# Modulation weights in buffers of their own, a reordered opening, and layer 1's recurrence values formed side by side

## The chip, the cores and the metric

The kernel runs on one core of one Trainium2 chip. The metric is the device time of one execution in microseconds (us); lower is better. The span in a profile is the part of that time between the first and the last instruction of the profiled execution.

## The reference

The reference is a block of two layers (`DEPTH` = 2) for a stream of 512 latent tokens and 256 context tokens, `D_MODEL` = 1024, all in float32. What is computed, cut to what matters here:

```python
silu_c, silu_cc = jax.nn.silu(c), jax.nn.silu(c_ctx)
for l in range(DEPTH):
    mod_lat = jnp.split((silu_c @ ada_w[l] + ada_b[l])[:, None, :], 6, axis=-1)   # ada_w[l]: 1024 x 6144
    mod_ctx = jnp.split(silu_cc @ ada_w[l] + ada_b[l], 6, axis=-1)
    z_lat = jnp.split(_modulate(x, norm1_w[l], mod_lat[0], mod_lat[1]) @ w_in[l], SPLIT_POINTS, axis=-1)
    z_ctx = ...                                  # the same for the context tokens
    # three mixers: gated recurrence (reads q, f, i, g columns of z), neighbourhood attention, short convolution
    x = x + mod_lat[2] * _branch_merge(...)      # three branch gates, branch projections, w_out
    x = x + mod_lat[5] * _sq_relu_mlp(_modulate(x, norm2_w[l], mod_lat[3], mod_lat[4]), mlp_w1[l], mlp_w2[l])
    ...                                          # the context tokens likewise, in layer 0 only
# _modulate(x, w, shift, scale) = rmsnorm(x) * w * (1 + scale) + shift
```

So the six modulation vectors of a layer (shift, scale and gate of the mixers, 0 to 2; shift, scale and gate of the MLP, 3 to 5) come from a 1024 x 6144 matrix times two vectors, and each is needed at a different place of the layer. The recurrence's values are the 512 `i` columns of `w_in`.

## The kernel before

**Products.** Each float32 product is made of three products of reduced inputs: a weight slab (128 x 1024, fetched as one transfer of 512 KB) is split into `wh` (copied by ScalarE, L205) and `wl` (what is left, made by VectorE, L206); activations likewise into `Hh` and `Hl`, or, inside the MLP, into the two halves of a tile `S`. `fm` (L224) then issues, for each of 8 blocks of the contracted dimension, `wh` x hi, `wh` x lo and `wl` x hi: 24 matrix instructions for 512 latent columns (tile `pl`) and 24 for 256 context columns (tile `pc`). This pair is called a step below. `tm_in` (L247) has the roles turned round: tokens are stationary, and 256 columns of weights stream past.

**Slabs.** `slab_plan` (L25) lists all slabs in the order of use. `next_w` (L209) hands out slab n, has slab n+1 split and the transfers up to slab n+3 issued, and then, if its argument `step` is true, advances the modulation stream by one item. Raw slabs lie in three buffers with the tag `raw` (L177). A slab's pair lies in `wh` and `wl` (two buffers each); a few named slabs use other tiles (`slabs_in`, L89).

**The modulation stream.** `ada_stream` (L352) works through items of 512 KB, each a quarter of the columns of one modulation vector and half of the contracted dimension. At its step i it issues item i's transfer into a `raw` buffer, multiplies item i-1 on VectorE (`ada`, L376: for each of four blocks and each of one or two rows one SCALAR_TENSOR_TENSOR, L387, the first one L385; after each second item a transpose and a reduction, L394 and L395), and closes a column quarter with a small TensorE product (`ada_sum`, L399). Layer 0's stream (vectors 2, 4, 3, 5) runs from the convolution stage on; layer 1's (1, 0, 2, 4, 3, 5) from the last four slabs of the first quarter of layer 0's MLP hidden units on. For layer 0, and for vectors 0 and 1 of layer 1, there are two rows (latent and context), for the others of layer 1 one.

**The opening.** Vectors 0 and 1 of layer 0 are needed at once. `start` (L299) computes them on TensorE: `ada_block` (L270) fetches 512 KB (8 blocks of 128 x 128, rows of 512 bytes) for each of 8 column blocks and 2 vectors into a ring of six `S` tiles and issues its matrix instructions (L282); `ada_block_sum` (L286) closes a column block (L290, L292, L294, L296). Beside that `norm_sq` (L433) sums the squares of x over eight blocks (ScalarE L442, VectorE L443), `norm_rms` (L445) makes the reciprocal root (TensorE L452, a chain of thirteen small VectorE instructions, then L458 spreads it on a diagonal), `norm_bc` (L462) broadcasts it by TensorE (L466), and `norm_apply` (L472: L481, L483, L484) makes `Hh` and `Hl`. The first half of the recurrence's value columns is then formed block by block (L338) as `Hh` and `Hl` come.

**Between the layers.** `last_products` (L1080) ends layer 0's MLP with the context columns first, normalises these, and leaves the latent columns' normalisation as `pending`. In layer 1 `hgrn_v` (L492) calls `tm_in` once for each half of the 512 value columns; `tm_in` does the context tiles (t = 4, 5), then calls `settle`, which runs what is pending, then does the four latent tiles, the tile loop outside the loop over the contracted dimension. In `mlp` (L1117) the hidden units go in quarters e = 0 to 3: eight `mlp_w1` steps with the square (`square`, L1105: L1112 to L1115), then eight `mlp_w2` steps with the residual (L1027).

**Order.** The instructions are put in order per engine ahead of time, by a planner that follows the program's order, a priority, and its own estimate of when data is there. On the chip each engine and each issuing queue (SP issues nearly all transfers) runs its list strictly in order, so an instruction that waits holds all behind it.

## Time and profile before

| | |
|---|---|
| median of 3 runs | 2505.33 us (2498.78 to 2507.31) |
| the profiled execution's own time | 2507.57 us |
| its span | 2505.8 us |
| TensorE matrix instructions | 2459.6 us busy, 98% of the span |
| TensorE weight loads | 2111.3 us, 84% |
| VectorE (DVE) | 1475.4 us, 59% |
| ScalarE (ACT) | 812.6 us, 32% |
| mean transfer rate | 93 GB/s |

The profile gives, for each engine, the busy time; matrix instructions are pipelined and their ends are modelled, so an engine shown as busy can still lose time: the distance between the starts of two equal pieces of work tells more than the busy share. "Idle before, releaser" is the time for which an engine stood still ahead of an instruction, and what ended it. In a row of the timeline the columns are the start in us, the duration in us, the engine, the line, the operation, output<-inputs, the shapes and how many are merged in the row (x).

### The profile page before, as it was taken

Reading aid. Unit: us, or ns where it says so; the run is one execution under the profiler, and the core shown is the slowest. Engines: PE = TensorE matmul, PEld = TensorE weight load, DVE = VectorE, ACT = ScalarE, POOL = GpSimd, SP = SyncE. Lnnn points to the kernel's source line nnn. Section 1 sums busy time; section 2 is a strip of 40 time slices with the busy share of each in tenths; the row PEclk is TensorE's granted clock in tenths of the full one; section 3 lists DMA queues with packets and bytes.
Section 4 is the critical chain, followed back from the end, with each engine's and each line's share of the span. In section 5 each row is a group of like instructions: output and inputs, shape, how many; then the busy total and the mean of one; then the engine's idle time right before and its main releaser. Section 6 shows DMA issues by size and latency. Waiting matters only on the chain.

```text
span 2505.8 us, 40660 instructions
## 1 busy us (share of the span) xinstructions
PE 2459.6 (98%) x17040; PEld 2111.3 (84%) x17040; DVE 1475.4 (59%) x2952; ACT 812.6 (32%) x1435; POOL 28.0 (1%) x52
## 2 busy tenths in 40 slices
PE   7999999999999999999999999999999999999999
PEld 6888988888888888878888888888878888888887
DVE  6477867776664666675655464787653335634433
ACT  4334365321212233121222333445442223422322
POOL 0000000000000000000000000000000000000000
PEclk9999999999999999999999999999999999999999
DMA  8111112233334212333343222111222233222322
GB/s 267 60 44 45 51 53 69 77 118 118 93 118 143 76 60 85 116 113 125 120 132 119 93 76 74 52 61 49 66 74 97 97 126 108 77 94 93 101 93 93
DMA packets 112344, 233.32 MB, mean 93 GB/s; under 512 B 8224, under 2 KB 65824, under 8 KB 112160
## 3 DMA queue, kind: packets, MB, share of 16 engines
q1 hardware_dynamic: 111584, 229.14, 28.1%
q8 instruction: 134, 2.20, 0.4%
q10 hardware_dynamic: 576, 1.57, 0.2%
q14 instruction: 50, 0.41, 0.1%
HBM read 226.49 MB, written 4.19 MB: 92 GB/s over the span
## 4 chain that ended last, share of the span: by engine, by line
PE 86%; DVE 7%; DMA 5%; ACT 2%; issue 1%; SPq 0%; DVEq 0%; ACTq 0%
PE pl L239 55%; PE pc L239 15%; PE tp L263 4%; DMA ada<-in_ada_w 4%; PE pc L263 2%; DVE adac L387 2%; DVE wl L206 1%; PE av L853 1%; PE ho L645 1%; PE sc L888 1%; PE kvp L621 1%; PE ptp L934 1%; PE lv L551 1%; DVE S L590 1%; PE tp L338 1%
## 5 line engine op out<-in xcount | busy, mean ns | idle before, releaser
L205 ACT ACTIVATE wh<-raw 128x1024 fp32r<-128x1024 f32 x297 | 314.5, 1059 | 849.7 <-PE pl L239 379.2
L239 PE MATMUL pl<-Hh,wh 128*128 128x512 f32 (+1 forms) x1488 | 586.5, 394 | 0.5 <-DVE S L1002 0.5
L239 PE MATMUL pl<-Hh,wl 128*128 128x512 f32 (+1 forms) x1488 | 581.4, 391 | 3.9 <-DVE wl L206 3.9
L239 PE MATMUL pl<-Hl,wh 128*128 128x512 f32 (+1 forms) x1488 | 581.1, 391 | 0.0
L206 DVE TENSOR_TENSOR wl<-raw,wh 128x1024 fp32r<-128x1024 f32 x297 | 363.2, 1223 | 318.5 <-ACT wh L205 313.7
L239 PE MATMUL pl<-S,wh 128*128 128x512 f32 x1392 | 436.4, 395 | 2.9 <-ACT S L1114 2.8
L239 PEld LDWEIGHTS pl<-Hh,wl 128*128 128x128 f32 x1488 | 279.7, 188 | 67.8 <-DVE wl L206 7.0
L239 PEld LDWEIGHTS pl<-Hh,wh 128*128 128x128 f32 x1488 | 279.7, 188 | 57.0 <-issue 0.8
L239 PEld LDWEIGHTS pl<-Hl,wh 128*128 128x128 f32 x1488 | 279.8, 188 | 55.1 <-issue 0.5
L239 PEld LDWEIGHTS pl<-S,wh 128*128 128x128 f32 x1392 | 258.3, 188 | 57.8 <-ACT S L1114 3.2
L239 PE MATMUL pl<-S,wl 128*128 128x512 f32 x696 | 273.8, 393 | 0.0
L387 DVE SCALAR_TENSOR_TENSOR adac<-ada,sc,adac 128x256 f32<-128x256 f32 x448 | 196.4, 481 | 119.4 <-DMA ada<-in_ada_w 116.6
L239 PE MATMUL pc<-Hh,wh 128*128 128x256 f32 x872 | 244.2, 280 | 0.8 <-ACT wh L205 0.6
L239 PE MATMUL pc<-Hh,wl 128*128 128x256 f32 x872 | 244.2, 280 | 0.2 <-DVE wl L206 0.2
L239 PE MATMUL pc<-Hl,wh 128*128 128x256 f32 x872 | 244.2, 280 | 0.0
L239 PEld LDWEIGHTS pc<-Hh,wh 128*128 128x128 f32 x872 | 164.5, 189 | 5.8 <-ACT wh L205 0.8
L239 PEld LDWEIGHTS pc<-Hl,wh 128*128 128x128 f32 x872 | 164.6, 189 | 4.4 <-DVE Hl L484 0.2
L1027 DVE SCALAR_TENSOR_TENSOR S<-pl,mod,S 128x512 f32<-128x512 f32 (+1 forms) x80 | 59.2, 740 | 180.2 <-PE pl L239 180.1
L239 PEld LDWEIGHTS pc<-Hh,wl 128*128 128x128 f32 x872 | 164.3, 188 | 1.0 <-issue 0.4
L239 PEld LDWEIGHTS pl<-S,wl 128*128 128x128 f32 x696 | 131.0, 188 | 30.4
L239 PE MATMUL pc<-S,wh 128*128 128x256 f32 x688 | 127.1, 285 | 0.0
L239 PEld LDWEIGHTS pc<-S,wh 128*128 128x128 f32 x688 | 111.5, 192 | 4.4
(269 smaller groups left out, 3131.7 us busy)
## 6 DMA issues: line engine op xcount, KB each, us to landing
raw<-in_w SPq DMA_DIRECT2D x304, 512.0 KB, 3.3
ada<-in_ada_w SPq DMA_DIRECT2D x80, 512.0 KB, 4.1
S<-in_ada_w SPq DMA_DIRECT2D x16, 512.0 KB, 7.3
B<-in_bias SPq DMA_DIRECT2D x16, 448.0 KB, 4.0
S<-in_xT SPq DMA_DIRECT2D x12, 384.0 KB, 6.0
xs<-S SPq DMA_DIRECT2D x8, 256.0 KB, 2.0
S<-xs SPq DMA_DIRECT2D x8, 256.0 KB, 4.6
out<-S SPq DMA_DIRECT2D x8, 256.0 KB, 2.0
```

Source lines behind the costliest of these rows:

```text
L205: self.nc.scalar.activation(hi, r, AF.Copy)
L206: self.nc.vector.tensor_tensor(lo, r, hi, op=ALU.subtract)
L239: nc.tensor.matmul(p, lhsT=W[:, s], rhs=X[:, t0:t0 + n], start=k == 0 and i == 0, stop=k == nk - 1 and i == 2)
L263: nc.tensor.matmul(o[t], lhsT=X[:, t * 128:t * 128 + 128], rhs=W[:, k4 * 256:k4 * 256 + 256], start=piece == 0 and k4 == 0 and i == 0, sto ...
L338: nc.tensor.matmul(o[t], lhsT=X[:, t * 128:t * 128 + 128], rhs=W[:, c], start=k == 0 and i == 0, stop=k == 7 and i == 2)
L387: nc.vector.scalar_tensor_tensor(out=acc[:, row, :], in0=w, scalar=s, in1=acc[:, row, :], op0=ALU.mult, op1=ALU.add)
L551: nc.tensor.matmul(p[32 * i:32 * i + 32, c * 32:c * 32 + 32], lhsT=lhs(o), rhs=rhs(o), start=True, stop=True, tile_position=(0, 32 * i))
L590: nc.vector.tensor_tensor(qv, qv, tv, op=ALU.mult)
L621: nc.tensor.matmul(kvp[:, i * P:(i + 1) * P], lhsT=kt[:, slots[qd, c]], rhs=vh(c), start=True, stop=True)
L645: nc.tensor.matmul(po[:, i * P:(i + 1) * P], lhsT=lh, rhs=rh, start=n == 0, stop=n == len(mms) - 1)
L853: nc.tensor.matmul(po[64 * pr:64 * pr + 64, o:o + m], lhsT=nv[:, t * 256 + d0:t * 256 + d0 + 64], rhs=pts[pr][:, pc:pc + m], start=n == 0, ...
L1027: nc.vector.scalar_tensor_tensor(out=x, in0=p[:, :n], scalar=self.mod[l][:, m, j, r:r + 1], in1=x, op0=ALU.mult, op1=ALU.add)
```

## The change

1. **Modulation stream.** Its items get three buffers of their own (tag `adaw`) and no longer share `raw`; an item is multiplied two steps after its transfer is issued, no longer one; the weights are laid out on the host so that an item is one run of 4 KB in each partition, where it was four runs of 1 KB. A stream needs one step more. In the MLP the `mlp_w1` steps of e = 0 and 1 advance the stream only at odd f.
2. **Opening.** The identity matrix is fetched second, ahead of x. `sel` is reduced from it after the sums of squares. The first two slabs' transfers are issued behind the second modulation block's, no longer ahead of all. The blocks' transfers are 4 KB runs, where they were 512-byte rows. The diagonal of the reciprocal root is written in two instructions, the context part first.
3. **Layer 1's values.** `hgrn_v2` takes all four slabs at once (the two of the second half go into `S` tiles 7 to 10), does the context tiles of both column halves, then settles, then seven of the eight latent products side by side, with the loop over the contracted dimension outside, in seven PSUM tiles, and the eighth after them. The context results are staged in `S[6]` and copied by GpSimd.
4. The scratch that is set aside for GpSimd's transfers is made smaller, which leaves room for the three buffers.

```diff
@@ run
+            self.slabs_in.update({n: (8, 7) if w[2] else (10, 9) for n, w in enumerate(self.plan)
+                                  if w[:2] == ("w_in", 1) and w[4] == OFF["i"] + 256})
@@ consts
         nc.sync.dma_start(out=cc, in_=self.a["cc"])
+        self.ident = self.cst("ident", [P, P])
...
-        self.ident = self.cst("ident", [P, P])
-        self.sel = sb.tile([P, 32], F32, name="sel")
-        nc.vector.tensor_reduce(out=self.sel, ...)
@@ ada_block
-            nc.sync.dma_start(out=r, in_=self.a["ada_w"][0, :, f0:f0 + P].rearrange("(k p) f -> p k f", p=P))
+            nc.sync.dma_start(out=self.S[slot][:, 0:1024], in_=self.a["ada1"][j, 1 - m])
@@ start
-        self.dma_slab()
-        self.dma_slab()
         ring = [0, 1, 8, 9, 10, 6]
         mp = {0: self.ada_block(0, ring)}
         self.norm_begin()
         for j in range(8):
             self.norm_sq(j, 0, T)
-        dg = self.norm_rms(0, T)
+        self.sel = self.sb.tile([P, 32], F32, name="sel")
+        nc.vector.tensor_reduce(out=self.sel, ...)
+        dg = self.norm_rms(0, T, ((512, 256), (0, 512)))
         mp[1] = self.ada_block(1, ring)
+        self.dma_slab()
+        self.dma_slab()
@@ ada_stream
-        for i in range(len(todo) + 3):
-            if i > 2 and todo[i - 3][2] == 1:
-                self.ada_sum(l, *todo[i - 3][:2], ahead.pop(i - 3))
+        for i in range(len(todo) + 4):
+            if i > 3 and todo[i - 4][2] == 1:
+                self.ada_sum(l, *todo[i - 4][:2], ahead.pop(i - 4))
             if i < len(todo):
                 m, c, kg = todo[i]
-                r = self.raw(f"ada{l}_{m}_{c}_{kg}")
...
+                r = self.sb.tile([P, 1024], F32, tag="adaw", bufs=3, name=f"ada{l}_{m}_{c}_{kg}")
+                self.nc.sync.dma_start(out=r, in_=self.a["ada2"][l, m, c, kg])
                 ahead[i] = r
-            if 0 < i <= len(todo):
-                m, c, kg = todo[i - 1]
+            if 1 < i <= len(todo) + 1:
+                m, c, kg = todo[i - 2]
                 with self.tc.high_priority(offset=-30):
-                    ahead[i - 1] = self.ada(l, m, kg, ahead.pop(i - 1))
+                    ahead[i - 2] = self.ada(l, m, kg, ahead.pop(i - 2))
@@ norm_rms
+        for p0, pn in parts or ((0, n),):
...                                              # one instruction per part in place of one in all
@@ new function, called by hgrn_v in layer 1
+    def hgrn_v2(self, l):
+        ws = [self.next_w("w_in", l, i == 0) for i in range(4)]
...
+        def part(g, t, k):
+            wh, wl = ws[2 * g + k // 4]
+            c = slice(k % 4 * 256, k % 4 * 256 + 256)
+            for i, (X, W) in enumerate(((self.Hh[k], wh), (self.Hl[k], wh), (self.Hh[k], wl))):
+                nc.tensor.matmul(o[g, t], lhsT=X[:, t * P:(t + 1) * P], rhs=W[:, c], ...)
...
+        self.new(6)
+        for g in range(2):
+            for t in (4, 5):
+                o[g, t] = self.pc()
+                for k in range(8):
+                    part(g, t, k)
+                evict(g, t, self.S[6][:, (t - 4) * 512 + g * 256:(t - 4) * 512 + g * 256 + 256])
+        self.settle()
+        side = [(0, t) for t in range(4)] + [(1, t) for t in range(3)]
+        for n, gt in enumerate(side):
+            o[gt] = (wide("pl", 2)[:, 0:256] if n < 2 else self.pc() if n < 4 else wide("m", 4)[:, 0:256])
+        for k in range(8):
+            for g, t in side:
+                part(g, t, k)
+        self.new(12, 13)
+        for t in (4, 5):
+            nc.gpsimd.tensor_copy(self.vt(t), self.S[6][:, (t - 4) * 512:(t - 3) * 512])
+        for g, t in side:
+            evict(g, t, self.vt(t)[:, g * 256:(g + 1) * 256])
+        o[1, 3] = wide("pl", 2)[:, 0:256]
+        for k in range(8):
+            part(1, 3, k)
+        evict(1, 3, self.vt(3)[:, 256:512])
@@ mlp
-                self.square(ff, f, self.fm(self.next_w("mlp_w1", l), *X))
+                self.square(ff, f, self.fm(self.next_w("mlp_w1", l, e > 1 or f % 2 == 1), *X))
@@ _host
-    a["ada_w"] = g["ada_w"]
+    a["ada1"] = ...                              # vectors 1 and 0 of layer 0, one run of 4 KB per partition
+    a["ada2"] = ...                              # all items of the streams, one run of 4 KB per partition
@@ kernel
-    nc = _bacc.Bacc("TRN2", target_bir_lowering=False, num_devices=1)
+    nc = _bacc.Bacc("TRN2", target_bir_lowering=False, num_devices=1, dynamic_dma_scratch_size=1024)
```

More of the change, by code (lines that the diff above doesn't have):

```diff
@@ L118, in consts @@
         self.nw = self.cst("nw", [P, 2, DEPTH, 8])
-        self.ident = self.cst("ident", [P, P])
-        self.sel = sb.tile([P, 32], F32, name="sel")
-        nc.vector.tensor_reduce(out=self.sel, in_=self.ident[:, :].rearrange("p (g i) -> p i g", g=4), op=ALU.add,
-                                axis=mybir.AxisListType.X)
         self.mod = [sb.tile([P, 6, 8, 2], F32, name=f"mod{l}") for l in range(DEPTH)]
@@ L274, in ada_block @@
         for m in (1, 0):
-            self.new(ring[0])
-            r = self.S[ring[0]][:, 0:1024].rearrange("p (k f) -> p k f", k=8)
-            ring.append(ring.pop(0))
-            f0 = m * D + j * P
-            nc.sync.dma_start(out=r, in_=self.a["ada_w"][0, :, f0:f0 + P].rearrange("(k p) f -> p k f", p=P))
+            slot = ring.pop(0)
+            ring.append(slot)
+            self.new(slot)
+            r = self.S[slot][:, 0:1024].rearrange("p (k f) -> p k f", k=8)
+            nc.sync.dma_start(out=self.S[slot][:, 0:1024], in_=self.a["ada1"][j, 1 - m])
             for i in range(2):
@@ L308, in start @@
             self.norm_sq(j, 0, T)
-        dg = self.norm_rms(0, T)
+        self.sel = self.sb.tile([P, 32], F32, name="sel")
+        nc.vector.tensor_reduce(out=self.sel, in_=self.ident[:, :].rearrange("p (g i) -> p i g", g=4), op=ALU.add,
+                                axis=mybir.AxisListType.X)
+        dg = self.norm_rms(0, T, ((512, 256), (0, 512)))
         mp[1] = self.ada_block(1, ring)
+        self.dma_slab()
+        self.dma_slab()
         self.ada_block_sum(0, mp[0])
@@ L443, in norm_sq, with norm_rms @@
             nc.vector.tensor_tensor(acc, acc, sq, op=ALU.add)
-    def norm_rms(self, t0, n):
+    def norm_rms(self, t0, n, parts=None):
         nc = self.nc
@@ L457, in norm_rms @@
         self.rsqrt(y, v, tt)
-        nc.vector.tensor_tensor(dg.rearrange("p (t q) -> p t q", q=P), self.ident[:, :].unsqueeze(1).broadcast_to([P, nt, P]),
-                                y.unsqueeze(2).broadcast_to([P, nt, P]), op=ALU.mult)
+        for p0, pn in parts or ((0, n),):
+            d = dg[:, p0:p0 + pn].rearrange("p (t q) -> p t q", q=P)
+            nb = [P, pn // P, P]
+            nc.vector.tensor_tensor(d, self.ident[:, :].unsqueeze(1).broadcast_to(nb),
+                                    y[:, p0 // P:(p0 + pn) // P].unsqueeze(2).broadcast_to(nb), op=ALU.mult)
         return dg
@@ L490, in ap, with evict @@
         return bass.AP(a.tensor, a.offset + off, [a.ap[0]] + [list(d) for d in dims])
+    def hgrn_v2(self, l):
+        nc = self.nc
+        ws = [self.next_w("w_in", l, i == 0) for i in range(4)]
+        o = {}
+        wide = lambda tag, bufs: self.ps.tile([P, 512], F32, tag=tag, bufs=bufs, name="tp")
+        def part(g, t, k):
+            wh, wl = ws[2 * g + k // 4]
+            c = slice(k % 4 * 256, k % 4 * 256 + 256)
+            for i, (X, W) in enumerate(((self.Hh[k], wh), (self.Hl[k], wh), (self.Hh[k], wl))):
+                nc.tensor.matmul(o[g, t], lhsT=X[:, t * P:(t + 1) * P], rhs=W[:, c],
+                                 start=k == 0 and i == 0, stop=k == 7 and i == 2)
+        def evict(g, t, dst):
+            if t % 2:
+                nc.scalar.activation(dst, o[g, t], AF.Copy)
+            else:
+                nc.vector.tensor_copy(dst, o[g, t])
+        self.new(6)
[21 more added lines that the diff above has]
+        evict(1, 3, self.vt(3)[:, 256:512])
     def hgrn_v(self, l, first=None):
+        if first is None:
+            return self.hgrn_v2(l)
         for g in range(2):
@@ L1158, in _host @@
     a["cc"] = np.stack([g["c"][0], g["c_ctx"]], -1).reshape(8, P, 2).transpose(1, 0, 2)
-    a["ada_w"] = g["ada_w"]
+    a["ada1"] = np.stack([g["ada_w"][0][:, m * D:(m + 1) * D].reshape(8, P, 8, P).transpose(2, 1, 0, 3).reshape(8, P, D)
+                          for m in (1, 0)], 1)
+    a["ada2"] = g["ada_w"].reshape(DEPTH, 2, 4, P, 6, 4, 256).transpose(0, 4, 5, 1, 3, 2, 6).reshape(DEPTH, 6, 4, 2, P, D)
     a["adab"] = g["ada_b"].reshape(DEPTH, 6, 8, P).transpose(3, 0, 1, 2)
```

4 lines of the change are left out of this document (removed).

## The prediction

> **What bounds the kernel now.** I read the page first, then TensorE's waits, then the transfers by stretch, then the timeline and the chain of waits at the three places that the diff touches.
>
> ```profile
> span 2505.8 us, 40660 instructions
> PE 2459.6 (98%) x17040; PEld 2111.3 (84%) x17040; DVE 1475.4 (59%) x2952; ACT 812.6 (32%) x1435; POOL 28.0 (1%) x52
> L387 DVE SCALAR_TENSOR_TENSOR adac<-ada,sc,adac 128x256 f32<-128x256 f32 x448 | 196.4, 481 | 119.4 <-DMA ada<-in_ada_w 116.6
> raw<-in_w SPq DMA_DIRECT2D x304, 512.0 KB, 3.3
> ```
>
> TensorE is busy for 98% of the span, so only places where it stands still or loses pace can give time back. VectorE waited 116.6 us for modulation items, but at 59% busy most of that costs nothing. The waits of TensorE itself (total, times, longest):
>
> ```profile
> PE adap L282 <- DMA S<-in_ada_w: 16.7, 2, 16.1
> PE pl L239 <- DVE wl L206: 3.9, 6, 1.1
> PE pc L263 <- ACT Hh L483: 2.9, 3, 1.6
> PE pl L239 <- ACT S L1114: 2.8, 1, 2.8
> ```
>
> The four belong to the opening, to the modulation stream, to the values of layer 1 and to the stream again: the places of the diff. Nothing else in it can gain more than a few us, and all other steps (the heads, attention, layer 1's MLP) are untouched.
>
> **Opening.** Stretches of the opening (length, busy time of TensorE, weight loads, VectorE, ScalarE, GpSimd; clock, transfer share, GB/s), then a row of the chain, then timeline rows:
>
> ```profile
> 3.00:9.00 6.00, 0.00 (x0) 0.00 (x0) 1.13 (x2) 4.42 (x6) 0.00 (x0) 1.00 1.03 412
> 14.00:30.00 16.00, 12.29 (x118) 10.12 (x122) 10.62 (x27) 5.63 (x9) 0.00 (x0) 1.00 1.18 291
> ```
>
> ```profile
> 2.10 7.90 DMA S<-in_xT
> ```
>
> ```profile
> 6.86 0.96 DVE L443 TENSOR_TENSOR S<-S,S 128x768 f32<-128x768 f32 x1 [2.48 <-ACT S L442]
> 11.73 0.37 DVE L121 TENSOR_REDUCE sel<-c_ident 128x32 f32<-128x128 f32 x1 [3.91 <-DMA c_ident<-in_ident]
> 15.01 1.22 DVE L206 TENSOR_TENSOR wl<-raw,wh 128x1024 fp32r<-128x1024 f32 x1
> 19.21 0.95 DVE L443 TENSOR_TENSOR S<-S,S 128x768 f32<-128x768 f32 x1
> 20.25 2.70 PE L452 MATMUL nms<-ones,S 128*128 128x2 f32 x12
> 25.40 0.96 DVE L458 TENSOR_TENSOR S<-c_ident,nst 128x768 f32<-128x768 f32 x1
> 26.26 1.08 PE L282 MATMUL adap<-S,sc 128*32 128x128 f32 x16
> 31.16 0.56 PE L338 MATMUL tp<-wh,Hh 128*128 128x256 f32 x1
> 58.82 0.28 PE L263 MATMUL tp<-wh,Hh 128*128 128x256 f32 x1
> ```
>
> x has landed by 10.0, but the last sum of squares ends at 20.2: VectorE stood 3.9 us for `sel`'s matrix and made two `wl` (2.4 us) in between. Both go. The seven sums then run back to back from 6.86: 6.86 + 7 x 1.05 = 14.2 (0.96 each, and some 0.1 between two). The row sums on TensorE follow at 14.2, or after the first two modulation halves: in place of 1 MB of slabs, these are next behind x; at 1.27 us per 512 KB (412 GB/s, the rate of x's 3 KB rows) and about 1.0 us to be told of, they are there at 13.0 and 14.3, and the second's product (1.08) ends at 15.4. So 4.9 to 6 us earlier than 20.25. The way from there to the first product took 31.16 - 20.25 = 10.9 us; the context part of the diagonal first takes 0.4 of L458's 0.96, so 10.4. First product: 24.6 to 25.8, **5.4 to 6.6 us earlier**.
>
> From the first product to the end of the opening, 58.82 - 31.16 = 27.7 us, it must be seen who is the bound:
>
> ```profile
> L282 PE MATMUL adap<-S,sc 128*32 128x128 f32 x160 | 6.4, 279 | 0.0
> L292 PE MATMUL adap<-sel,adac 128*128 128x2 f32 x24 | 3.4, 248 | 0.0
> ```
>
> The 144 value products (8 blocks x 6 tiles x 3) at 0.117 (their pace in layer 1, below) take 16.9; with 6.4 and 3.4, and about 1 us of changes between the kinds, that is TensorE's 27.7: it is the bound, not the transfers. So it all moves up by the earlier start, less two things. One or two modulation halves may fall behind the first product instead of ahead of it: 0 to 1.2 us. And TensorE is slow at first: twelve row sums took 2.70 us, eight at 1482 took 1.02 (row below), and the first product lasts 0.56 where later ones last 0.28; the dense work that ended this had begun at 26.3, 5 us before. If the first products now fall into such 5 us, they lose up to 2.5; I take 1. Opening: 6 - 1 = **5 us** (bounds 1 and 8; 8 if the row sums come first and nothing is lost).
>
> The Trainium skill (DMA: Bandwidth & Descriptors, section Specifications) has it that transfers of 512 bytes and more already run at line rate, by which the new layout would bring nothing. The trace disagrees: 291 GB/s with 512-byte rows against 412 with 3 KB rows. By the rule the two halves would be there at 13.6 and 15.4, the sum would be about 1 us less; I stay with the row.
>
> **Modulation stream.** The first eight `mlp_w1` steps of e = 1 and the step after them, in timeline and chain, then VectorE's groups from 1060 to 1134 (busy, mean ns | idle before, releaser) and the busy times of that stretch:
>
> ```profile
> 1060.05 0.50 PE L239 MATMUL pl<-Hh,wh 128*128 128x512 f32 x1
> 1133.66 0.50 PE L239 MATMUL pl<-S,wh 128*128 128x512 f32 x1
> 1141.59 1.65 PE L239 MATMUL pl<-S,wh 128*128 128x512 f32 x2 [2.81 <-ACT S L1114]
> ```
>
> ```profile
> 1148.41 5.54 PE pl L239 x24
> 1208.53 5.70 PE pl L239 x24
> 1242.17 5.72 PE pl L239 x24
> ```
>
> ```profile
> L387 DVE SCALAR_TENSOR_TENSOR adac<-ada,sc,adac 128x256 f32<-128x256 f32 x49 | 21.6, 480 | 11.3 <-DMA ada<-in_ada_w 11.2
> L385 DVE TENSOR_SCALAR adac<-ada,sc 128x256 f32<-128x256 f32 x6 | 2.0, 352 | 7.4 <-DMA ada<-in_ada_w 7.4
> ```
>
> ```profile
> 1060.00:1134.00 74.00, 70.13 (x425) 59.09 (x423) 51.95 (x111) 19.89 (x35) 0.00 (x0) 1.00 0.36 115
> ```
>
> A clean step is (1242.17 - 1208.53) / 4 = 8.41 us. The nine steps from 1060.05 to 1148.41 took 88.36 where 9 x 8.41 = 75.7: **12.7 us lost**. VectorE is why: in these 74 us it stood 18.6 us for items whose transfer could start only when a shared buffer came free; `wl` and the squares queue behind that. After the change an item is issued two steps (some 17 us) ahead, against 3.3 us for 512 KB, into a buffer that no slab needs; and only four of these eight steps bring an item, so about half of the 21.6 + 2.0 us goes as well: VectorE's 52 us of 74 become some 40 of 67. Both causes are removed. The half of the items that moves goes to the later quarters, where steps were clean with one item each. I take 11.5, and 0.1 to 0.2 us per step stay (bounds 4 and 13; 4 is what the list of waits gives for L206 alone).
>
> Layer 0's stream has the same waits on VectorE, but TensorE's list holds none that they cause; I take **1** (0 to 2).
>
> **Layer 1's values.** TensorE's timeline, then VectorE's groups from 1482 to 1496, then TensorE's from 1479.7, then SP's issue of the fourth slab:
>
> ```profile
> 1479.73 0.28 PE L263 MATMUL tp<-wh,Hh 128*128 128x256 f32 x1
> 1487.05 1.13 PE L466 MATMUL nbc<-S,ones 128*128 128x128 f32 x8 [0.40 <-DVE S L458]
> 1489.77 0.50 PE L263 MATMUL pc<-wh,Hh 128*128 128x256 f32 x2 [1.59 <-ACT Hh L483]
> 1495.50 0.50 PE L263 MATMUL pc<-wh,Hh 128*128 128x256 f32 x2 [0.63 <-ACT Hh L483]
> 1520.67 0.39 PE L239 MATMUL pl<-Hh,wh 128*128 128x512 f32 x1
> ```
>
> ```profile
> L481 DVE SCALAR_TENSOR_TENSOR S<-S,A,nbc 128x512 f32<-128x512 f32 x6 | 4.2, 743 | 1.3 <-PE nbc L466 1.3
> L484 DVE SCALAR_TENSOR_TENSOR Hl<-S,mod,Hh 128x512 fp32r<-128x512 f32 x5 | 3.6, 750 | 0.4
> ```
>
> ```profile
> L452 PE MATMUL nms<-ones,S 128*128 128x2 f32 x8 | 1.0, 251 | 0.0
> ```
>
> ```profile
> 1482.05 0.33 SPq L185 DMA_DIRECT2D raw<-in_w x1
> ```
>
> The stage takes 1520.67 - 1479.73 = 40.9 us. Of its 288 products (2 halves x 6 tiles x 24) 72 lie ahead of 1495.50; the other 216 follow in 25.17 us, 0.117 each. At this pace all are 33.7, row sums and broadcast 0.9 and 1.1: 35.7. At most 5.2 can be gained. The cover is there: the context tiles of both halves are 96 products = 11.2 us, up to about 1493, when blocks 0 and 1 (1.5 us each on VectorE, ready from 1489.7) lie ready; then 21 products per block (2.5 us) are slower than the 1.5. What is late next: the second half's slabs. They need tiles that the MLP holds until 1479.7, and the fourth's transfer is issued at 1482.05, when the second slab frees its buffer; 3.3 us, then 1.22 on VectorE and about as long on ScalarE, between the root chain's instructions: 1487.8 or later, where TensorE wants it at about 1487.5. Loss 0 to 2. The eighth product waits for a PSUM tile to be emptied, an estimate of 0.5 to 0.8 by the 128x512 instructions of 0.75 above. GpSimd's two copies are needed only by the first head's later half. I take **4** (1 to 5).
>
> **Sum.** 5 + 11.5 + 1 + 4 = 21.5 us. The profiled execution's own time is 2507.57 (span 2505.8 and 1.8 around it): 2486.1. It stands 2.2 above the median of the runs, 2505.33, so for a median 2483.8: **2484**. With all lower bounds 2499, with all upper ones 2477.
>
> **The rivals.** (a) *The opening gives nothing*: first products at half pace, and the planner puts the two `wl`, whose slabs now land later, into the root chain, so VectorE stands in wait of a slab as it did of `sel`: 2489. For: VectorE did hold `wl` at 15.01 ahead of a sum of squares. Against: the slabs land at about 17, ahead of the chain's end. The Trainium skill (TensorE: Matmul & The Clock Gate, Part 1) gives the half pace as the default until some 3.4 us of sustained work; the 5 us from 26.3 to 31.2 agree roughly. (b) *The stall in e = 1 stays*: it is the squares' own work, not the items; only 1 us of 11.5 comes: 2494. Against: 18.6 us of waits. (c) *Slower*: SP now waits for an `adaw` buffer, which comes free only when VectorE, at low priority, has done the item of three steps before, and the next slab's transfer is queued behind. Place: every step of both streams, 80 items. Price: the 3.9 us of 6 waits for `wl` in 8 steps, 0.5 per step, or 39 us, and the 12.5 of the stream are not gained: 2507.6 - 9 + 39, 2535 as a median. It decides once VectorE's work exceeds a step's 8.4; now 52 us in 8 steps are 6.5 each, so it should not.
>
> **How the numbers follow.** Forecast 0.70 (its own range 2477 to 2491), (a) 0.12, (b) 0.13, (c) 0.05. No change that can be told is within 0.3% of 2505.33, 2497.8 to 2512.8. The forecast, (a) and most of (b) lie below: faster 0.87; a tail of (b), with a weak opening: same 0.09; (c) and unforeseen order: slower 0.04. Range 2474 to 2498: from the sum of all upper bounds, with 3 more for the spread of the runs (2498.78 to 2507.31), to that of the lower ones.
>
> **What would show it.** After: no wait of DVE L387 on its transfers; e = 1's `mlp_w1` steps at 8.4 to 8.6 us; first value product at 24 to 26 us and the opening's last at 53 to 55; layer 1's value stage at 36 to 38 us. I am wrong if SP's slab issues move behind waits for `adaw`, if `wl` still releases TensorE in e = 1, or if the opening's end stays near 59.

## The result, and the profile after

| | before | after |
|---|---|---|
| median of the runs | 2504.51 us (4 runs) | 2485.82 us (2483.64 to 2487.41, 4 runs) |
| ratio, 95% interval | | 0.992 (0.9908 to 0.9932) |
| the profiled execution's own time | 2507.57 us | 2487.41 us |

The forecast was 2484 us, its range 2474 to 2498. The sum was made against a profiled execution, and between the two profiled ones lie 20.2 us of 21.5 forecast; between the medians lie 18.7 us. First the head of the page after, VectorE's two groups that wait for items:

```profile
span 2485.6 us, 40668 instructions
PE 2454.5 (99%) x17040; PEld 2108.5 (85%) x17040; DVE 1486.0 (60%) x2953; ACT 818.1 (33%) x1435; POOL 29.6 (1%) x54
...
L387 DVE SCALAR_TENSOR_TENSOR adac<-ada,sc,adac 128x256 f32<-128x256 f32 x448 | 201.8, 479 | 14.4 <-DMA ada<-in_ada 8.4
...
L385 DVE TENSOR_SCALAR adac<-ada,sc 128x256 f32<-128x256 f32 x64 | 22.1, 347 | 1.8 <-DMA ada<-in_ada 1.5
```

VectorE's idle time ahead of L387 was 119.4 us and is 14.4. With L385, whose row of before is the next one, 204 us of waiting became 16. Only some 10 us of these 188 reached the end, as the experiments show.

```profile
L385 DVE TENSOR_SCALAR adac<-ada,sc 128x256 f32<-128x256 f32 x64 | 20.8, 351 | 84.5 <-DMA ada<-in_ada_w 84.5
```

The first two of TensorE's own waits after (total, times, longest):

```profile
PE adap L282 <- DMA S<-in_ada: 12.8, 1, 12.8
PE lv L600 <- DVE S L639: 4.3, 8, 0.9
```

The rows of `pl` on `wl` and on the square are gone; what stands below the opening is attention and recurrence, which the diff doesn't touch.

Below are the distances between fixed places of TensorE's list, before, after, and the gain. Each row runs from the mark named to the next; the marks are starts of instructions in the timeline, taken from one profiled execution of each kernel. The opening's end is the start of the first value product behind the opening's own (L263); the prediction and the expectations call this mark the opening's last value product.

| stage | before | after | gain | forecast |
|---|---|---|---|---|
| start to the opening's end | 58.82 | 55.17 | 3.65 | 5 |
| from there to the first `mlp_w1` step of e = 1 (layer 0's stream) | 1001.23 | 1000.99 | 0.2 | 1 |
| eight `mlp_w1` steps of e = 1 | 73.61 | 66.82 | 6.8 | together 11.5 |
| the step behind them | 14.59 | 8.61 | 6.0 | |
| from there to the end of layer 0 | 331.48 | 332.36 | -0.9 | |
| layer 1's values | 40.93 | 36.19 | 4.7 | 4 |
| the rest | 980.90 | 981.27 | -0.4 | 0 |

**Opening.** Timeline of the changed kernel:

```profile
0.73 3.84 ACTq L112 DMA_DIRECT2D S<-in_xT  x4
...
4.60 1.28 ACT L117 ACT_TABLE_LOAD   x1 [4.60 <-DMA S<-in_xT]
...
7.99 0.96 DVE L443 TENSOR_TENSOR S<-S,S 128x768 f32<-128x768 f32 x1 [1.67 <-ACT S L442]
...
14.37 0.96 DVE L443 TENSOR_TENSOR S<-S,S 128x768 f32<-128x768 f32 x1
...
15.55 1.01 PE L292 MATMUL adap<-sel,adac 128*128 128x2 f32 x4 [0.50 <-ACT adac L290]
...
16.43 2.70 PE L452 MATMUL nms<-ones,S 128*128 128x2 f32 x12
...
22.61 0.16 DVE L294 TENSOR_TENSOR mod<-adap,c_adab 128x4 f32<-128x4 f32 x1 [1.47 <-PE adap L292]
...
24.09 2.35 DVE L206 TENSOR_TENSOR wl<-raw,wh 128x1024 fp32r<-128x1024 f32 x2
...
26.12 1.08 PE L282 MATMUL adap<-S,sc 128*32 128x128 f32 x16
...
27.58 0.57 PE L341 MATMUL tp<-wh,Hh 128*128 128x256 f32 x2
...
28.77 0.65 PE L282 MATMUL adap<-S,sc 128*32 128x128 f32 x16
...
55.17 0.28 PE L263 MATMUL tp<-wh,Hh 128*128 128x256 f32 x1
```

The sums are now one every 1.06 us without a gap, but begin at 7.99, not at 6.86. The first value product is 3.6 us earlier than before (31.16), where 5.4 to 6.6 were forecast; from it to the end nothing is lost (27.59 us, 27.66 before). What lies ahead of the row sums (L452) is in the chain of waits, of the changed kernel, then of before:

```profile
2.11 6.22 DMA S<-in_xT
...
8.35 5.57 DMA S<-in_ada
...
13.96 1.13 PE adap L282 x16
...
15.11 0.40 ACT adac L290
```

```profile
10.45 7.29 DMA S<-in_ada_w
```

In both kernels the chain runs through the transfer of the first block's second modulation half, its product, ScalarE's copy of it and the block's closing (L292); the row sums stand behind this closing in TensorE's list. The half lands at 13.92 us, before at 17.74: 3.82 us earlier, and the row sums come 3.82 us earlier (16.43, before 20.25).

**Stream.** The chain of waits through e = 1, then the larger of VectorE's two groups and all engines' busy times over the eight steps:

```profile
1056.33 5.60 PE pl L239 x24
...
1089.80 5.49 PE pl L239 x24
...
1123.14 5.57 PE pl L239 x24
```

```profile
L387 DVE SCALAR_TENSOR_TENSOR adac<-ada,sc,adac 128x256 f32<-128x256 f32 x27 | 12.0, 476 | 0.1
```

```profile
1056.10:1123.00 66.90, 66.90 (x403) 58.60 (x403) 40.88 (x81) 23.21 (x38) 0.00 (x0) 1.00 0.28 95
```

Four steps take 33.5 and 33.3 us, 8.4 and 8.3 each; TensorE is busy without a break, VectorE for 40.9 of 66.9 us and with no wait for an item.

**Values.** Timeline of layer 1's value stage:

```profile
1467.69 1.22 DVE L206 TENSOR_TENSOR S<-raw,S 128x1024 fp32r<-128x1024 f32 x1
...
1474.97 0.73 ACT L486 ACTIVATE Hh<-S,mod 128x512 fp32r<-128x512 f32 x1 [3.61 <-DVE S L484]
...
1477.40 0.28 PE L506 MATMUL tp<-wh,Hh 128*128 128x256 f32 x1
...
1500.15 0.40 PE L239 MATMUL pl<-Hh,wh 128*128 128x512 f32 x1
```

All four slabs are split by 1468.9, 8.5 us ahead of the first product of a latent tile at 1477.40; block 0 is there at 1475.7. TensorE waits for nothing.

### The profile page after: what moved, and what is told of

Same layout as the page of the kernel before. It is cut to its first block, busy times and chain, and to the rows that moved or that the text cites. A ratio compares the mean times of both kernels' runs of the same rounds, so it can differ in the third digit from the quotient of the medians.

```text
span 2485.6 us, 40668 instructions
## 1 busy us (share of the span) xinstructions
PE 2454.5 (99%) x17040; PEld 2108.5 (85%) x17040; DVE 1486.0 (60%) x2953; ACT 818.1 (33%) x1435; POOL 29.6 (1%) x54
## 4 chain that ended last, share of the span: by engine, by line
PE 94%; DVE 3%; ACT 2%; DMA 1%; issue 1%; SPq 0%; DVEq 0%; ACTq 0%; POOL 0%
PE pl L239 60%; PE pc L239 18%; PE tp L263 3%; PE pc L263 2%; PE sc L937 1%; PE ho L694 1%; PE av L902 1%; PE ptp L983 1%; PE kvp L670 1%; PE pc L506 1%; PE tp L506 1%; PE lv L600 1%; DMA B<-in_bias 1%; DVE S L639 1%; PE tp L341 1%
## 5 line engine op out<-in xcount | busy, mean ns | idle before, releaser
L387 DVE SCALAR_TENSOR_TENSOR adac<-ada,sc,adac 128x256 f32<-128x256 f32 x448 | 201.8, 479 | 14.4 <-DMA ada<-in_ada 8.4
L1076 DVE SCALAR_TENSOR_TENSOR S<-pl,mod,S 128x512 f32<-128x512 f32 (+1 forms) x80 | 59.2, 740 | 180.6 <-PE pl L239 180.5
```

The costliest lines, as they stand in the source:

```text
L387: nc.vector.scalar_tensor_tensor(out=acc[:, row, :], in0=w, scalar=s, in1=acc[:, row, :], op0=ALU.mult, op1=ALU.add)
L1076: nc.vector.scalar_tensor_tensor(out=x, in0=p[:, :n], scalar=self.mod[l][:, m, j, r:r + 1], in1=x, op0=ALU.mult, op1=ALU.add)
```

## The experiments

All start from the changed kernel. They ran on three chips, where the kernel before took 2507.88 (the first four), 2507.49 (the next four) and 2507.9 us (the last four). "e = 1" is the eight steps plus the step behind them; opening and values are the stages of the table above. The stage columns come from one profiled execution of each kernel.

| kernel | median us | ratio to before, 95% | e = 1 | opening | values |
|---|---|---|---|---|---|
| a1_every_step | 2488.45 | 0.9912 to 0.9942 | 67.81 + 8.61 | 57.21 | 35.44 |
| a2_shared_buffers | 2489.69 | 0.9919 to 0.9949 | 67.31 + 8.46 | 56.30 | 35.41 |
| a3_old_values | 2495.18 | 0.9939 to 0.9969 | 66.82 + 8.61 | 56.44 | 40.94 |
| a4_old_order_opening | 2488.75 | 0.9911 to 0.9944 | 66.82 + 8.64 | 58.02 | 35.41 |
| b0_shared_every | 2496.60 | 0.9946 to 0.9975 | 69.33 + 11.11 | 57.47 | 35.43 |
| b2_own_lead1_every | 2488.02 | 0.9910 to 0.9940 | 68.10 + 8.47 | 56.30 | 35.43 |
| c1_sel_loaded | 2487.28 | 0.9906 to 0.9939 | 66.82 + 8.64 | 56.03 | 36.20 |
| c2_norm_first | 2490.15 | 0.9916 to 0.9946 | 66.82 + 8.64 | 55.59 | 36.20 |
| d1_stream_before | 2501.20 | 0.9965 to 0.9987 | 74.18 + 11.91 | 55.56 | 36.23 |
| d2_skip_only | 2491.72 | 0.9916 to 0.9946 | 68.74 + 8.46 | 56.34 | 36.23 |
| b1_rows_512 | 2487.90 | 0.9902 to 0.9931 | 66.82 + 8.61 | 57.05 | 35.44 |
| after_again | 2489.12 | 0.9906 to 0.9936 | 66.82 + 8.61 | 56.56 | 35.41 |

### Which part of the stream's edit counts

The stream's change has three parts that can work alone: skipped steps, own buffers (with a longer lead), longer runs.

**a1_every_step**: own buffers, lead of two steps and long runs, but an item at each step.

```diff
-                self.square(ff, f, self.fm(self.next_w("mlp_w1", l, e > 1 or f % 2 == 1), *X))
+                self.square(ff, f, self.fm(self.next_w("mlp_w1", l), *X))
```

> The changed kernel, but every mlp_w1 step advances the modulation stream again, as in the kernel before; the buffers of its own and the lead of two steps stay. Theory (the shared buffers and the short lead were the cause; VectorE has room for an item in each step): the eight mlp_w1 steps of e = 1 with the step behind them stay within 2 us of the 75.5 us that nine clean steps take, VectorE waits for no item there, time 2485 to 2488 us. Rival (too many items beside the squares were the cause): 4 us or more come back there, time 2490 to 2498 us.

The eight steps and the one behind take 76.42 us, and VectorE stands for under 1 us ahead of its items, as the theory had it (the median is 0.5 us above its range). One us slower in e = 1 (67.81), one faster later: the stretch before layer 1 takes 68.40 us against 69.54 in after_again. VectorE is not the reason, for no item is multiplied in that stretch in either kernel. It is TensorE's own work that moves, the small products that close a column quarter: a1 has 32 of them in the eight steps of e = 1 and none in that stretch, after_again 16 and 24. The skipped steps add nothing that can be told once the items have buffers of their own.

**a2_shared_buffers**: shared buffers and a lead of one step, skipped steps and long runs kept. (All indices of the stream's loop that the change raised by one are set back.)

```diff
-                r = self.sb.tile([P, 1024], F32, tag="adaw", bufs=3, name=f"ada{l}_{m}_{c}_{kg}")
+                r = self.raw(f"ada{l}_{m}_{c}_{kg}")
...
-                m, c, kg = todo[i - 2]
+                m, c, kg = todo[i - 1]
...
```

> The changed kernel, but the stream's items lie in the slabs' raw buffers again and are multiplied one step after their transfer is issued; the skipped steps and the 4 KB runs stay. Theory (the shared buffers are the cause): VectorE waits for items again, 4 us or more per item with the slab transfers beside them; in e = 1 with half of the items some 3 to 7 us of the 13 us are lost again, time 2489 to 2493 us. Rival (the skipped steps alone do it): under 1.5 us lost, time 2485 to 2487 us.

```profile
L387 DVE SCALAR_TENSOR_TENSOR adac<-ada,sc,adac 128x256 f32<-128x256 f32 x34 | 14.8, 477 | 9.0 <-DMA ada<-in_ada 9.0
...
L385 DVE TENSOR_SCALAR adac<-ada,sc 128x256 f32<-128x256 f32 x4 | 1.2, 350 | 4.1 <-DMA ada<-in_ada 4.1
```

```profile
1057.90:1125.20 67.30, 67.30 (x405) 58.98 (x403) 43.85 (x89) 22.48 (x38) 0.00 (x0) 1.00 0.35 110
```

I had thought that shared buffers would bring several us of loss back. They bring the waits back, 13.1 us on VectorE, and TensorE hardly notices: 67.31 in place of 66.82, with 24 closing products in place of 16. VectorE's work and its waits, 43.9 + 13.1 = 57.0, stay under the 67 us that TensorE needs. So the rival holds in e = 1 (0.3 us lost over the nine steps), although the median lies in the theory's range.

**b0_shared_every**: both undone, long runs kept. **b2_own_lead1_every**: own buffers, lead of one step, an item at each step. Both are combinations of the two diffs above.

> The changed kernel with the stream's buffers, its lead of one step and its step at every mlp_w1 as before; only the 4 KB runs of the items stay. After the two kernels that undid one of these each lost about 1 us, there are two theories. Theory A (either cure is enough: TensorE loses time only where VectorE's work and its waits for items together exceed the eight steps' 67 us, some 52 + 18 us before): with both undone the eight mlp_w1 steps of e = 1 take 72 to 74 us and the step behind them 12 to 15 us; time 2497 to 2501 us. Theory B (the stall was the transfers' layout in runs of 1 KB): they take under 69 and 9 us; time 2488 to 2490 us.

> The changed kernel with a step at every mlp_w1 and a lead of one step, but in the stream's own buffers. If the sharing alone makes VectorE wait (an item lands within 3.3 us of its issue, a step lasts 8.4 us): waits for items under 5 us in the eight mlp_w1 steps of e = 1, which take 67.5 to 68.5 us; time 2487 to 2490 us. If the short lead makes it wait: 10 us of waits or more and steps of 70 us or more; time 2492 us or more.

b0 lies between its two theories: it loses 2.5 us in the eight steps and 2.5 in the next. b2 loses 1.3 and nothing; TensorE waits nowhere there, and 32 of the closing products lie in the eight steps, as in a1. So buffers of their own are a cure by themselves, and the second step of lead is worth nothing measurable. But b0 is 7.8 us better than the kernel before (88.20), though it differs from it in the stream only by its runs of 4 KB.

**d1_stream_before**: the stream wholly as before. **d2_skip_only**: as d1, with the skipped steps. To the diff below come those of a2 and, in d1, of a1.

```diff
-                self.nc.sync.dma_start(out=r, in_=self.a["ada2"][l, m, c, kg])
+                f0 = m * D + c * 256
+                self.nc.sync.dma_start(
+                    out=r[:, :].rearrange("p (k f) -> p k f", k=4),
+                    in_=self.a["ada_w"][l, kg * 512:(kg + 1) * 512, f0:f0 + 256].rearrange("(k p) f -> p k f", p=P))
```

> The changed opening and layer-1 values, the modulation stream wholly as before: shared slab buffers, multiplied one step after the issue, an item at each of the eight steps, runs of 1 KB. It differs from the kernel with shared buffers, each step and 4 KB runs (b0) only in the runs. Theory: the run length is the third cause; with 1 KB runs an item lands about 0.8 us later (4.1 against 3.3 us), VectorE waits some 8 times longer for its item, and its work and waits pass the 67 us that TensorE needs: the eight mlp_w1 steps of e = 1 take 73 to 74 us and the step behind them 14 to 15, as before, against 69.3 and 11.1 in b0; median 2500 to 2505. Rival: the layout is worth nothing here, and what b0 gained over the kernel before came from the order around it (opening, values): 69 to 70 and 10.5 to 11.5, median within 2 us of b0's 2496.6.

> The changed opening and layer-1 values; of the stream's change only the skipped steps (items at odd f in e = 0 and 1): shared buffers, one step ahead, 1 KB runs. Theory: VectorE's sum decides, and half the items halve both its work for them and its waits: 44 us of work and some 13 to 16 us of waits stay under TensorE's 67: eight steps in 67 to 68 us, 8.4 to 8.8 for the next, median 2488 to 2491, so that the one-line edit brings nearly all of the stream's gain. Rival: a wait of one item longer than VectorE's slack in a step (about 2 us) holds up wl for TensorE whatever the sum is: 69 us or more and 10 or more behind, median 2494 or more.

VectorE's groups and the busy times over the eight steps, of d1, then of b0:

```profile
L390 DVE SCALAR_TENSOR_TENSOR adac<-ada,sc,adac 128x256 f32<-128x256 f32 x50 | 22.0, 479 | 11.5 <-DMA ada<-in_ada_w 11.3
...
L388 DVE TENSOR_SCALAR adac<-ada,sc 128x256 f32<-128x256 f32 x6 | 2.0, 353 | 6.9 <-DMA ada<-in_ada_w 6.9
```

```profile
1056.80:1131.00 74.20, 69.78 (x424) 58.71 (x423) 52.56 (x111) 19.91 (x35) 0.00 (x0) 1.00 0.37 114
```

```profile
L387 DVE SCALAR_TENSOR_TENSOR adac<-ada,sc,adac 128x256 f32<-128x256 f32 x46 | 20.3, 480 | 10.5 <-DMA ada<-in_ada 10.3
...
L385 DVE TENSOR_SCALAR adac<-ada,sc 128x256 f32<-128x256 f32 x6 | 2.0, 352 | 5.6 <-DMA ada<-in_ada 5.6
```

```profile
1059.70:1129.00 69.30, 68.63 (x424) 59.39 (x417) 49.90 (x107) 19.86 (x35) 0.00 (x0) 1.00 0.38 121
```

TensorE's waits for `wl` from 1040 to 1200 us in d1 (total, times, longest):

```profile
PE pl L239 <- DVE wl L206: 4.6, 8, 0.9
```

In d1, 52.6 of work and 18.4 of waiting for items make 71.0 us, more than the 67.8 that TensorE takes for the same steps when no item is late (a1). VectorE, "busy" for 71%, sets the pace, and TensorE waits for its `wl` eight times. In b0 the sum is 49.9 + 16.1 = 66.0, and TensorE waits for `wl` once, 0.6 us, and for a square, 1.5 us. The run length, the only edit between the two, takes off 5.65 us (74.18 + 11.91 against 69.33 + 11.11). In these stretches an item landed a median of 4.6 us after its issue in d1 and 4.2 in b0, some 0.4 on eight items; how this grows to 5.65 is not shown. The size is rough too, since it rests on one profile of each, from two chips, and d1's profiled execution is the fastest of its eight (2498.38). d1's theory holds but for the step behind, 11.91 in place of 14 to 15; its rival, that the layout is worth nothing, falls.

d2 lies between its two expectations: 68.74 + 8.46, a sum of 45.4 + 9.0 + 4.8 = 59.2 of work and waiting for items, but TensorE still waits twice for `wl`, 1.1 us in all. The sum decides most, a single late item a little; it is no sharp threshold, as b0 loses time at 66.0. The one-line edit brings 8.9 us of the 10.7 between d1 (86.09) and after_again (75.43).

### The opening

**a4_old_order_opening**: old places of the identity, of `sel` and of the slabs, one diagonal instruction; 4 KB runs kept.

```diff
-        self.ident = self.cst("ident", [P, P])
...
         self.nw = self.cst("nw", [P, 2, DEPTH, 8])
+        self.ident = self.cst("ident", [P, P])
+        self.sel = sb.tile([P, 32], F32, name="sel")
...
+        self.dma_slab()
+        self.dma_slab()
...
-        dg = self.norm_rms(0, T, ((512, 256), (0, 512)))
+        dg = self.norm_rms(0, T)
```

**b1_rows_512**: the new order, with 512-byte rows.

```diff
-            nc.sync.dma_start(out=self.S[slot][:, 0:1024], in_=self.a["ada1"][j, 1 - m])
+            nc.sync.dma_start(out=r, in_=self.a["ada_w"][0, :, m * D + j * P:m * D + j * P + P].rearrange("(k p) f -> p k f", p=P))
```

**after_again**: no edit.

> The changed kernel, but with the opening's old order (slabs first, identity matrix after x, sel ahead of the sums of squares, the diagonal in one instruction); the 4 KB runs of the opening's modulation blocks stay. Theory (order and not transfer rate sets the opening): the first value product comes at 30 to 31.2 us and the opening's last at 57.5 to 59 us, time 2488 to 2490 us. Rival (the faster transfers brought it): the opening's last value product stays under 56 us, time 2486 us.

> The changed kernel, only the opening's modulation weights fetched again in rows of 512 bytes. Theory (transfer bound at the start): halves at 1.8 us in place of 1.25, so the first row sums or the block closings shift by 0.5 to 2 us and the opening ends 0.5 to 2 us later than the changed kernel's of this chip; median 0 to 2 us above it. Rival (TensorE is the bound from the first product on, and the first product hangs on VectorE's and TensorE's order): the opening's end within 1 us of the changed kernel's, and no difference in the median that can be told.

> The changed kernel unaltered, as the reference for the other three on this chip and to see how far its opening's end scatters from run to run. If the 55.2 to 57.5 us over kernels with the same opening are scatter of when x lands, this run lies in 55 to 57.5 too and not at 55.17; if they come from the edits, it repeats 55.2 within 0.3. The e = 1 steps: 66.8 and 8.6; the value stage 35.4 to 36.2; median about 0.992 of the kernel before.

Timeline of after_again, then the stretch from 12 to 26 us of after_again and of b1:

```profile
17.71 2.70 PE L452 MATMUL nms<-ones,S 128*128 128x2 f32 x12
...
56.56 0.28 PE L263 MATMUL tp<-wh,Hh 128*128 128x256 f32 x1
```

```profile
12.00:26.00 14.00, 10.62 (x105) 8.64 (x106) 8.27 (x25) 5.27 (x8) 0.00 (x0) 1.00 1.02 407
```

```profile
12.00:26.00 14.00, 10.27 (x103) 8.29 (x104) 8.04 (x25) 5.39 (x8) 0.00 (x0) 1.00 1.13 336
```

The unaltered kernel ends its opening at 56.56 here, not at 55.17: it scatters. Over the nine profiles with this opening (after, after_again, a1, a2, a3, b0, b2, d1, d2) the end lies at 55.17 to 57.47, mean 56.4. The gain is 2.4 us on the mean against before and 1.7 against a4, whose theory holds (first value product at 30.41, end at 58.02): order sets the opening.

The chains of waits show through what. The product of the first block's second modulation half begins, as soon as the halves have landed, at 17.79 us in before and 17.39 in a4, where the slabs' transfers go ahead of them, and at 13.96 to 16.43 in the nine. In all fourteen profiles the opening ends 40.6 to 41.5 us behind this point. The scatter comes from ahead of it: the transfer of x that precedes the half in the chain ends at 8.33 in after and 9.76 in after_again. The 512-byte rows cost nothing that can be told: in b1 that product begins at 15.60, inside the scatter, the opening's end is 0.5 us later, and the median 1.2 us lower, although the rate in that stretch was 336 GB/s against 407.

**c1_sel_loaded**: what holds the first sum? The identity is again fetched behind x, and `sel` is loaded as a small constant, so that nothing waits for the identity early. **c2_norm_first**: in addition, the closing of the first modulation blocks and the splits of the slabs are tied behind the norm's steps on their engines (the diff shows block 0; block 1 and the two splits are tied likewise).

```diff
-        self.ident = self.cst("ident", [P, P])
...
         self.nw = self.cst("nw", [P, 2, DEPTH, 8])
+        self.sel = self.cst("sel", [P, 32])
+        self.ident = self.cst("ident", [P, P])
```

```diff
-        self.ada_block_sum(0, mp[0])
+        with self.tc.issue_after(self.last_ms.ins), self.tc.issue_after(self.last_dg.ins):
+            self.ada_block_sum(0, mp[0])
...
```

> The changed kernel with the identity matrix fetched behind x again, and sel fetched as a constant of its own (16 KB more), so that VectorE makes nothing of the identity matrix ahead of the root's diagonal. Theory (the identity matrix ahead of x holds up x's transfers and with them ScalarE's start and the first sum of squares, which came at 8.0 to 9.7 us where it came at 6.8 us): first sum at 6.8 to 7.0 us, row sums on TensorE at 15 to 16.5 us, the opening's last value product at 53.5 to 55 us; time 2486 to 2488 us where the changed kernel would have 2488 to 2489 us on the same chip. Rival (x's arrival is the chip's own scatter): first sum still at 8 us or later, the opening's end at 55.2 to 57.2 us.

> As the kernel with sel fetched as a constant, and the order on the engines tied down in the opening: the row sums ahead of the first modulation block's closing product on TensorE, the whole chain of the root ahead of the blocks' closing on VectorE, and the first slabs' wl behind the first block's L481. Theory (these three cost the first product 1.0, 1.9 and 1.0 us in the changed kernel): row sums at 14.5 to 15.5 us, the first value product 8.5 to 9.5 us behind them where it was 11.2 us, the opening's last value product at 50.5 to 53 us; time 2483 to 2486 us. Rival (TensorE's work after the first product grows by as much, since the modulation blocks move behind it, or it runs at half pace there): the opening's end no earlier than with sel fetched alone, within 0.7 us.

The first sum is back at 7.20 and 6.68. The opening's end hardly moves, 56.03 and 55.59, inside the scatter, and both theories miss. In both kernels the product of the second modulation half begins at 14.89, inside the range of the others. In c1 the last sum of squares ends at 14.5, but the row sums begin only at 17.35, behind that half's product and the block's closing. Timeline of c2, which takes the closing out of the way:

```profile
15.90 2.72 PE L454 MATMUL nms<-ones,S 128*128 128x2 f32 x12
...
22.10 1.01 PE L293 MATMUL adap<-c_sel,adac 128*128 128x2 f32 x4 [0.50 <-ACT adac L291]
...
25.80 2.20 PE L471 MATMUL nbc<-S,ones 128*128 128x128 f32 x10
...
28.96 0.48 PE L343 MATMUL tp<-wh,Hh 128*128 128x256 f32 x2
```

The row sums begin 1.8 us earlier than in after_again, but the way from them to the first product is 13.1 us in place of 11.15: two blocks' closings and four halves lie ahead of the larger part of the broadcast in TensorE's list, where it was one closing and three halves. The time taken out ahead of the norm comes back inside it.

### Layer 1's values

**a3_old_values**: `hgrn_v` as before in layer 1, and without the two places in `S` tiles for its slabs.

```diff
-        if first is None:
-            return self.hgrn_v2(l)
```

> The changed kernel, but layer 1's values are formed as before, one column half after the other, the tile loop outside. Theory (TensorE waits for the blocks of Hh in turn): the stage from the first value product to the first head is 40.9 us again where it is 36.2 us, TensorE waits about 4 us for L486 and L487, time 2490 to 2491 us. Rival (the profile of before had caught a bad moment and the gain is elsewhere): the stage stays under 38 us, time 2486 us.

The stage takes 40.94 us again, 4.7 to 5.5 more than in all kernels with `hgrn_v2` (35.41 to 36.23). TensorE waits in it for blocks of `Hh` (2.9 us) and `Hl` (0.9 us) as in before; in none of the kernels with `hgrn_v2` does it wait in this stage. The median, above the range expected, is 5.5 to 6.7 us above those of a1, a2 and a4 on the same chip; what it has beyond the stage is not traced.

## Why the prediction was right, and where it was not

The time was right, and so was where most of it comes from. That it came so close is in part luck: between the two profiles the stream gave 1.3 us more than forecast and the opening 1.35 less, and some 2 us of what the stream gave are a dip of the granted clock in the profile of before.

**Stream, forecast 11.5, 12.8 between the two profiles.** The step "VectorE is why" holds: d1 has the old loss back, with VectorE's work and waits for items at 71.0 us where TensorE needs 67.8. The profile of before contains something that is no part of the change. Its stretch behind the eight steps, then the same stretch of d1:

```profile
1134.00:1148.20 14.20, 11.33 (x48) 9.43 (x47) 7.00 (x15) 3.17 (x6) 0.00 (x0) 0.76 0.46 146
```

```profile
1131.00:1142.90 11.90, 9.56 (x56) 7.47 (x53) 6.98 (x16) 3.17 (x6) 0.00 (x0) 1.00 0.45 136
```

The granted clock was 0.76 there, (1 - 0.76) x 14.2 = 3.4 us at most of lost pace; d1, at 1.00, took 2.1 us less in the two stretches (86.09 against 88.20). What the edit itself brings is 86.09 - 75.43 = 10.7. Some 1 us of this comes back: "The half of the items that moves goes to the later quarters, where steps were clean with one item each" was put at nothing, but the stretch ahead of layer 1 took 69.5 us in place of 68.4 to 68.6, in each kernel that skips steps about 1 us more than in those that don't (a1, b0, b2, d1: 68.4). The 24 closing products on TensorE that now lie there are what differs; those of the stream are the same in number, so their time is moved and not gained (read from the counts; no run moves them alone). The forecast named two causes, buffers and number of items. There is a third that it left out, the run length (5.65 us between d1 and b0), and the three don't add: skipped steps alone bring 8.9, own buffers with the long runs alone 9.5 (b2: 76.57). Each brings VectorE's sum under TensorE's need, after which the others have little left to save.

**Opening, forecast 5, 3.65 in this profile and 2.4 on the mean of nine.** That the row sums hang on the second modulation half was in the working, and the half landed at 13.92, where 14.3 was forecast. (The terms given, 10.0 + 2 x 1.27 + 1.0, make 13.5; the other 0.8 us of the 14.3 have no term.) On the mean of the nine its product begins at 15.2, behind transfers of x that scatter.

The working failed at three steps. First, the row sums were put at 15.4, right behind that half's product; ScalarE's copy and the closing of block 0 (L292, 1.01 us) lie between them: 16.43. Second, "10.4" from there to the first product was 11.15: the root chain stood 1.47 us for L294, whose TensorE product was late, and the two `wl` (2.35 us) lie ahead of `norm_apply`, as rival (a) had it, though at a price of less than 1 us. These two, 1.03 and 0.75 us, give the first product at 27.58 where 25.8 was the later bound. Third, "run back to back from 6.86": the identity went ahead of x in SP's queue, and I counted what that frees but not what it moves. ScalarE's four issues for x then last until 4.57, where before they ended by 2.63, and its table load starts at 4.60, not 2.66. The first sum comes at 7.99 and, where the next block of x lands late as well, up to 9.74. c1 shows the identity as the cause, 7.20 with it behind x, and also that this alone costs the opening's end nothing that can be told. Rows of before that go with 0.73 and 4.60 of the changed kernel's timeline:

```profile
0.73 1.90 ACTq L108 DMA_DIRECT2D S<-in_xT  x4
...
2.66 1.28 ACT L113 ACT_TABLE_LOAD   x1 [2.66 <-issue]
```

The 1 us taken off for cold first products did not occur: the 27.6 us from the first product to the end are the same as before. A half takes 1.08 us at 26.12 and 0.65 at 28.77, so the full pace comes about with the first product; in before it is 1.08 at 29.70 and 0.64 at 32.49. The Trainium skill (TensorE: Matmul & The Clock Gate, Part 1) has the half pace until some 3.4 us of sustained work. The trace agrees only in part: from 15.55 to 21.0 TensorE works end to end, 5.4 us, and at 26.12 a half still takes 1.08; no run tells whether products of two columns, 3.5 us of this stretch, count as such work. The rate with 4 KB runs was as the rows of x had it, 416 GB/s from 12 to 26 us in the profile after. b1 shows that the length of the runs brought nothing here that can be told; what decides is when the first block's halves have landed, and the order of the transfers sets that (17.39 in a4).

**Layer 1's values, forecast 4, measured 4.7 (and 5.5 at the faster pace below).** The loss set aside for late slabs was 0: the last of the four transfers was issued at 1460.78, 3.2 us ahead of the stage, and all was split by 1468.9, 5 us into it, where I had put the fourth 8.1 us in (1487.8). The tiles were taken for held until the MLP's last step; the first of them was being filled at 1442.77. The eighth product waits for nothing.

**Layer 0's stream, forecast 1, measured 0.2.** Over the fourteen profiles this stage scatters from 999.2 to 1002.5 us, so neither figure can be told from nothing. Most of VectorE's waits lay there and went, and no gain shows, as TensorE's list of waits had said.

**The rivals.** (b), that the squares' own work is the stall, falls with a1 and b2: without the items' waits the steps are clean, with the squares unchanged and an item at each step. (a) falls too: the opening gave 2.4 us on the mean, though less than forecast. (c) is there as a mechanism and costs nothing. SP's wait for an `adaw` buffer, after (total, times, longest):

```profile
SPq L365 <- DVE adac L387: 166.8, 74, 4.1
```

I had written that I would be wrong if slab issues moved behind such waits. They do, at 74 of 80 items, and no slab is late for it: no `wl` releases TensorE in e = 1. The sign of failure was badly chosen; a wait on the issuing queue counts only where the transfer behind it is late.

## What to carry to other kernels

Add to an engine's work, stage by stage, its waits for transfers that only its own progress sets going, and compare the sum with what the other engine needs: at 52.6 us of work in 74, with 18.4 of such waits, VectorE set the pace, and of 188 us of waiting removed some 10 counted. Leave out waits that lead back to the other engine, and expect some loss already a few us below the limit. Any edit that brings this sum well under the other engine's need gives nearly the whole gain, so try the smallest first. In an opening, follow the chain through the transfers before reordering the work: here the end followed the landing of the first block in every profile, and two reorderings of the work around the norm (c1, c2) moved the end by nothing that can be told. An opening should be judged over several profiles when it scatters by 2 us.

## What the runs showed of the hardware that was not expected

- **One small transfer ahead on SP lengthens the issues on another queue.** With the identity (128 x 128, 64 KB) ahead of x, ScalarE's four issues for x took 3.84 us (3.43 to 3.84 in the ten profiles with this order), with it behind x 1.90 (c1: 1.86). SP's own four became shorter, 2.38 us in after and 3.42 in before. No row says why.
- **The same product has two paces at full clock.** In the value stage fifteen products of 128 x 256 took 1.77 us in one profile and 1.70 in another of the same kernel (0.118 and 0.1133 each), which is all the difference between 36.19 and 35.41 us. In the changed kernel's chain both occur within the stage, 3.41 us for thirty and then 1.77 for fifteen. No row says why; this stays open. The chain of after, then of after_again:

```profile
1479.11 1.77 PE tp L506 x15
```

```profile
1481.41 1.70 PE tp L506 x15
```

- **Short dips of the granted clock.** Besides the one of before in e = 1, eight of the fourteen profiles, of both kernels among them, have one in layer 1's second norm (0.86 over 12 us in the row below, of the changed kernel); five (a4 among them, 1.00 there) have none, and d2 has one elsewhere. At (1 - 0.86) x 12 = 1.7 us it is as large as most differences between the medians of the kernels that were near each other.

```profile
2120.00:2132.00 12.00, 10.72 (x70) 9.88 (x69) 11.07 (x35) 6.32 (x12) 0.00 (x0) 0.86 0.36 128
```
